# Row standard deviation: hand synchronisation, a ScalarE loop, aligned code, new last pieces and a VectorE transpose

## Chip, cores and metric

One core of one Trainium2 chip. The metric is the device time of one execution in microseconds (us), given as a median over several executions. Each execution also has a span, from its first to its last instruction as the profiler records it. In the two kernels compared the time is 1.7 to 2 us longer than the span, and that difference will matter. One execution per run was kept as a full profile. All executions compared here were classed as fast, except two single looks, whose state is unknown, as that of a single execution on one core always is.

## The reference

```python
# x: 8192 x 8192 float32, normally distributed
def reference(x):
    return np.std(x, axis=1)
```

The input is 268.4 MB, the output 32 KB. The kernel reads the input once.

## The kernel before

Thirty groups of 256 rows, 64 KB per partition each, pass through three buffers. VectorE sums each row, ScalarE squares and sums it. The last group and the four last blocks of 128 rows are divided otherwise: ScalarE takes 3072 columns of each row, VectorE makes batch-norm statistics of the rest. In the very last block, of which ScalarE takes 2048 columns, the input arrives in seven pieces, so that little work is left when the last byte lands. In the list of pieces, each pair is (columns that arrive, columns of them for ScalarE). A framework puts in all the waits. The parts that matter here:

```python
    for g in range(G - 1):
        xt = bulk.tile([P, 2 * C], FP32, name="xt")
        nc.sync.dma_start(out=xt, in_=xg[g])
        nc.vector.reduce_sum(out=s_all[:, 2 * g:2 * g + 2],
                             in_=xt.rearrange("p (j m) -> p j m", j=2),
                             axis=mybir.AxisListType.X)
        for j in range(2):
            squash(xt[:, j * C:(j + 1) * C], C, ACTF.Square, q_all[:, 2 * g + j:2 * g + j + 1])


    H = C // 2
    pieces = [(2048, 512), (2048, 512), (2048, 1024), (1024, 0), (512, 0), (256, 0), (256, 0)]
    # ... loads of the last group (xt_l), of rows 1 and 2 (xt_a), of row 3 in two halves ...
    c0 = C
    for n, _ in pieces:
        nc.sync.dma_start(out=xt_b[:, c0:c0 + n], in_=xt_rows[0][:, c0 - C:c0 - C + n])
        c0 += n
    # ... statistics of those rows; GpSimd joins the shares; TensorE transposes the results ...
    c0, k, j = C, 0, 0
    for n, a in pieces:
        src = xt_b[:, c0:c0 + n]
        if a:
            cnt, mean, m2v = (tri[:, 3 * j + i:3 * j + i + 1] for i in range(3))
            nc.gpsimd.memset(cnt, float(a))
            squash(src[:, 0:a], a, ACTF.Copy, mean, scale=1.0 / a)
            squash(src[:, 0:a], a, ACTF.Square, q_p[:, j:j + 1])
            # ... GpSimd turns ScalarE's two sums into (count, mean, squares) ...
        k = bn_cols(tri[:, 3 * n_act:], k, src[:, a:n])
        c0 += n

    nc.vector.bn_aggr(out=fin[:, 0:2], in_=tri)
    ps_t = psum.tile([TR, P], FP32)
    nc.tensor.transpose(ps_t, fin[:, 1:1 + TR], ident)
    std_t = stats.tile([TR, P], FP32)
    nc.scalar.activation(out=std_t, in_=ps_t, func=ACTF.Sqrt)
    nc.scalar.dma_start(out=out_t, in_=std_t)
```

## Time and profile before

| | before |
|---|---|
| time, first session, as it stood when the prediction was made | 630.96 us median of 3 (630.87 to 631.29) |
| span of the profiled execution (its time: 631.55 us) | 629.7 us |
| input queue, share of the 16 DMA engines | 98.8% |
| VectorE, ScalarE busy | 86%, 71% |

The page of the kernel before, first part: span, busy time and share of each engine, busy tenths of the DMA engines in 40 slices, and the DMA queues.

```profile
span 629.7 us, 466 instructions
...
PE 1.0 (0%) x3; PEld 0.2 (0%) x3; DVE 539.3 (86%) x99; ACT 449.4 (71%) x157; POOL 7.3 (1%) x44
...
DMA  9999999999999999999999999999999999999995
...
q1 hardware_dynamic: 5949, 268.47, 98.8%
q14 instruction: 4, 0.03, 0.0%
```

The input stream is what bounds the kernel: the DMA row is nine or more in every slice but the last. Queue 14 carries instructions. It has four packets in the span.

The chain of waits of the kernel before, in order of time (start, duration, what), beginning and end:

```profile
0.81 0.41 SPq L75
...
1.27 40.79 DMA xt<-in_x_dram
...
42.08 17.23 DVE s_all L76
...
59.37 41.02 DMA xt<-in_x_dram
...
584.49 37.31 DMA xt<-in_x_dram
...
621.83 1.29 DVE tri L68 x2
...
623.12 2.54 DVE tri L68 x5
...
625.76 0.56 DVE fin L187
...
626.36 0.39 PE ps_t L189
...
626.77 0.27 ACT std_t L191
```

A load takes 41 us from issue to landing because another, of 19.35 us, is served before it. A VectorE link of the chain only says which buffer came free; the DMA engines do not run dry meanwhile. From 621.83 us on it is different: VectorE works without a wait to 625.66, and then the output chain runs (aggregate, TensorE transpose, ScalarE square root).

The timeline of the kernel before, at its start and its end (start, duration, engine, line, operation; in brackets the idle time before and what ended it):

```profile
0.81 39.57 SPq L75 DMA_DIRECT2D xt<-in_x_dram  x4
0.87 0.06 DVE L49 MEMSET warm<- 128x1 f32 x1 [0.87 <-PEq L207]
...
22.75 17.22 DVE L76 TENSOR_REDUCE s_all<-xt 128x2 f32<-128x16384 f32 x1 [21.82 <-DMA xt<-in_x_dram]
...
42.08 17.22 DVE L76 TENSOR_REDUCE s_all<-xt 128x2 f32<-128x16384 f32 x1 [2.12 <-DMA xt<-in_x_dram]
...
621.83 3.82 DVE L68 BATCH_NORM_STATS2 tri<-xt 128x6 f32<-128x512 f32 x7 [0.42 <-DMA xt<-in_x_dram]
...
625.76 0.55 DVE L187 BATCH_NORM_AGGREGATE fin<-tri 128x2 f32<-128x87 f32 x1
...
627.07 0.55 ACTq L192 DMA_DIRECT2D out_dram<-std_t  x1
```

The first load is issued at 0.81 us, and the last store at 627.07, 2.64 us before the span ends.

Under the views lie the records of single DMA packets and landings. A load of 128 partitions runs on 16 engines and has 16 landings (those of the first load of the kernel before lie between 22.09 and 22.72 us); the kernel waits for all of them. For the argument below, the last landing is the one that counts. "Eighth landing" is the eighth of the 16 in order of time and stands for a typical engine.

### The profile page before, as it was taken

The page shows a single profiled execution, that of the slowest core. Times are in us where ns is not written, and L with a number is a line of the kernel's source. Part 1 is how long each engine was busy: PE and PEld are TensorE (multiplying, and loading weights), DVE is VectorE, ACT ScalarE, POOL GpSimd, SP SyncE. Part 2 cuts the span into 40 slices and gives each one's busy share as a digit, 9 for nine tenths or more (in the row PEclk, how much of TensorE's full clock was granted, in tenths as well). Part 3 has the DMA queues.
Part 4 walks back from the last instruction along what each step waited for, and adds up shares of the span by engine and source line. Part 5 has one row for each costly group of instructions (what it writes and reads, how often), then busy time and mean ns, then how long its engine had stood idle before and what let it go on. Part 6 is the DMA issues. An engine that isn't in the chain of part 4 may idle for free.

```text
span 629.7 us, 466 instructions
## 1 busy us (share of the span) xinstructions
PE 1.0 (0%) x3; PEld 0.2 (0%) x3; DVE 539.3 (86%) x99; ACT 449.4 (71%) x157; POOL 7.3 (1%) x44
## 2 busy tenths in 40 slices
PE   0000000000000000000000000000000000000000
PEld 0000000000000000000000000000000000000000
DVE  0588988889988889888898888998888988889897
ACT  0566886667966669766688666796666976668885
POOL 0000000000000000000000000000000000000002
DMA  9999999999999999999999999999999999999995
GB/s 400 408 458 404 462 400 466 400 466 400 466 400 466 400 466 400 466 400 466 400 466 400 466 400 466 400 466 404 462 412 454 416 450 429 437 437 429 419 411 240
DMA packets 5961, 268.50 MB, mean 426 GB/s; under 512 B 675, under 2 KB 965, under 8 KB 1221
## 3 DMA queue, kind: packets, MB, share of 16 engines
q1 hardware_dynamic: 5949, 268.47, 98.8%
q14 instruction: 4, 0.03, 0.0%
q10 hardware_dynamic: 8, 0.00, 0.0%
HBM read 268.44 MB, written 0.03 MB: 426 GB/s over the span
## 4 chain that ended last, share of the span: by engine, by line
DMA 71%; DVE 28%; SPq 0%; issue 0%; PE 0%; ACT 0%; DVEq 0%
DMA xt<-in_x_dram 71%; DVE s_all L76 27%; DVE tri L68 1%; SPq L95 0%; SPq L92 0%; SPq L75 0%; DVE fin L187 0%; PE ps_t L189 0%; ACT std_t L191 0%; DVEq L187 0%
## 5 line engine op out<-in xcount | busy, mean ns | idle before, releaser
L76 DVE TENSOR_REDUCE s_all<-xt 128x2 f32<-128x16384 f32 x29 | 499.4, 17220 | 82.3 <-DMA xt<-in_x_dram 82.3
L63 ACT ACTIVATE dump<-xt 128x8192 uint8<-128x8192 f32 (+4 forms) x76 | 440.4, 5794 | 174.3 <-DMA xt<-in_x_dram 173.0
L68 DVE BATCH_NORM_STATS2 bn<-xt 128x6 f32<-128x512 f32 x50 | 30.1, 675 | 3.1 <-DMA xt<-in_x_dram 3.1
L63 ACT ACTIVATION_READ_ACCUMULATOR dump<-xt 128x1 f32 x76 | 14.2, 186 | 0.0
L68 DVE BATCH_NORM_STATS2 tri<-xt 128x6 f32<-128x512 f32 (+1 forms) x13 | 7.4, 635 | 0.4 <-DMA xt<-in_x_dram 0.4
L106 POOL TENSOR_TENSOR m<-s_all 128x58 f32<-128x58 f32 x1 | 0.3, 282 | 581.3 <-DVE s_all L76 581.3
L120 DVE BATCH_NORM_AGGREGATE agg<-bn 128x2 f32<-128x60 f32 x5 | 2.1, 425 | 0.2
L191 ACT ACTIVATE std_t<-ps_t 4x128 f32<-4x128 f32 x1 | 0.3, 266 | 2.6 <-PE ps_t L189 2.6
L50 ACT ACT_TABLE_LOAD x1 | 1.3, 1283 | 0.8 <-PEq L207 0.8
L148 PE MATMUL ps_g<-ident,vN 128*30 128x128 f32 x2 | 0.6, 410 | 600.0 <-POOL vN L137 600.0
L49 DVE MEMSET warm<- 128x1 f32 x1 | 0.1, 59 | 0.9 <-PEq L207 0.9
L187 DVE BATCH_NORM_AGGREGATE fin<-tri 128x2 f32<-128x87 f32 x1 | 0.5, 548 | 0.1
L176 POOL TENSOR_TENSOR m_p<-tri 128x1 f32<-128x1 f32 x3 | 0.6, 193 | 0.8 <-ACT dump L63 0.8
L178 POOL TENSOR_TENSOR tri<-q_p,m_p 128x1 f32<-128x1 f32 x3 | 0.6, 189 | 1.2 <-ACT dump L63 1.1
L177 POOL TENSOR_TENSOR m_p<-m_p,tri 128x1 f32<-128x1 f32 x3 | 0.6, 190 | 0.2
L189 PE MATMUL ps_t<-ident,fin 128*4 128x128 f32 x1 | 0.4, 373 | 25.8 <-DVE fin L187 25.8
L152 ACT ACTIVATE std_g<-ps_g 30x128 f32<-30x128 f32 x2 | 0.4, 256 | 0.0
L159 POOL TENSOR_TENSOR s_all<-s_all,s_half 128x1 f32<-128x1 f32 x1 | 0.2, 190 | 17.7 <-ACT dump L63 17.7
L129 POOL TENSOR_TENSOR ug<-agg 128x2 f32<-128x2 f32 x1 | 0.2, 194 | 13.9 <-DVE agg L120 13.9
L148 PEld LDWEIGHTS ps_g<-ident,vN 128*30 128x30 f32 x2 | 0.1, 114 | 600.0 <-POOL vN L137 600.0
L108 POOL TENSOR_TENSOR vN<-q_all,m 128x58 f32<-128x58 f32 x1 | 0.3, 307 | 0.1
L173 POOL MEMSET tri<- 128x1 f32 x3 | 0.3, 98 | 0.0
(30 smaller groups left out, 5.3 us busy)
## 6 DMA issues: line engine op xcount, KB each, us to landing
xt<-in_x_dram SPq DMA_DIRECT2D x2, 4096.0 KB, 36.0
xt<-in_x_dram SPq DMA_DIRECT2D x2, 2048.0 KB, 29.0
xt<-in_x_dram SPq DMA_DIRECT2D x3, 1024.0 KB, 36.3
xt<-in_x_dram SPq DMA_DIRECT2D x1, 512.0 KB, 38.1
xt<-in_x_dram SPq DMA_DIRECT2D x30, 40.8
xt<-in_x_dram SPq DMA_DIRECT2D x1, 256.0 KB, 29.3
xt<-in_x_dram SPq DMA_DIRECT2D x2, 128.0 KB, 17.3
out_dram<-std_g SPq DMA_DIRECT2D x1, 30.0 KB, 10.2
```

The source lines that it names most:

```text
L50: nc.scalar.activation(out=warm, in_=warm, func=ACTF.Sqrt)
L63: nc.scalar.activation(out=dump[:, 0:n], in_=src, func=func, scale=scale, accum_out=acc)
L68: nc.vector.bn_stats(out=bn[:, k * SD:(k + 1) * SD], in_=src[:, d0:min(n, d0 + F)])
L76: nc.vector.reduce_sum(out=s_all[:, 2 * g:2 * g + 2], in_=xt.rearrange("p (j m) -> p j m", j=2), axis=mybir.AxisListType.X)
L120: nc.vector.bn_aggr(out=agg[:, r, :], in_=bn)
L148: nc.tensor.transpose(ps_g[:, j, :], vg[:, :, j], ident)
L152: nc.scalar.activation(out=std_g[:, :, j], in_=ps_g[:, j, :], func=ACTF.Sqrt, scale=1.0 / N)
L176: nc.gpsimd.tensor_mul(m_p[:, j:j + 1], mean, mean)
L177: nc.gpsimd.tensor_mul(m_p[:, j:j + 1], m_p[:, j:j + 1], cnt)
L178: nc.gpsimd.tensor_sub(m2v, q_p[:, j:j + 1], m_p[:, j:j + 1])
L187: nc.vector.bn_aggr(out=fin[:, 0:2], in_=tri)
L189: nc.tensor.transpose(ps_t, fin[:, 1:1 + TR], ident)
```

## The change

The intent: take instruction fetches out of the input stream (ScalarE loops over the groups, and the code of ScalarE and VectorE is aligned by `addr_align(128)`), end with less work after the last byte (new pieces), and shorten the output chain (VectorE transposes the last block's result instead of TensorE). For the loop, all the waits are written by hand. The diff is 439 lines; its core, with cuts marked and three comments added:

```diff
+    ctx.enter_context(tc.tile_critical())       # hand-synchronised from here
+    std_kernel(ctx, tc.nc, x, out)
 ...
+    for eng in (nc.vector, nc.scalar):
+        eng.addr_align(128, offset=0, max_nops=0)
 ...
-    pieces = [(2048, 512), (2048, 512), (2048, 1024), (1024, 0), (512, 0), (256, 0), (256, 0)]
+    pieces = [(3072, 768), (1536, 1024), (1024, 0), (1024, 512), (512, 0), (512, 0), (512, 0)]
 ...
-        for j in range(2):
-            squash(xt[:, j * C:(j + 1) * C], C, ACTF.Square, q_all[:, 2 * g + j:2 * g + j + 1])
+    with nc.scalar.Fori(0, LOOPS * 2 * NBUF, 2 * NBUF) as col:
+        for b in range(NBUF):
+            nc.scalar.wait_ge(token, 1)
+            nc.scalar.nop().then_inc(token, -1)
+            for j in range(2):
+                squash(buf[b][:, j * C:(j + 1) * C], C, ACTF.Square,
+                       q_all[:, bass.ds(col + (2 * b + j), 1)]).then_inc(row_done, 1)
+                nc.scalar.wait_ge(row_done, 1)
+                nc.scalar.nop().then_inc(row_done, -1)
+            nc.scalar.nop().then_inc(squared, 1)
 ...
+    for g in range(G - 1):                      # TensorE passes on landed data and free buffers
+        ...
+        T.need(V, v_group[g])
+        ...
+        nc.tensor.nop().then_inc(free, 1)
 ...
-    nc.vector.bn_aggr(out=fin[:, 0:2], in_=tri)
-    ps_t = psum.tile([TR, P], FP32)
-    nc.tensor.transpose(ps_t, fin[:, 1:1 + TR], ident)
-    std_t = stats.tile([TR, P], FP32)
-    nc.scalar.activation(out=std_t, in_=ps_t, func=ACTF.Sqrt)
-    nc.scalar.dma_start(out=out_t, in_=std_t)
+    # rows 1 to 3 are transposed, rooted and stored before this point
+    aggregated(fin[:, 0:2], tri)
+    V.need(V, V.n)
+    v_fin = V.did(nc.vector.transpose(out=tr, in_=fin[:, 1:33]))
+    A.need(V, v_fin)
+    A.did(nc.scalar.activation(out=std_l, in_=tr, func=ACTF.Sqrt))
+    A.need(A, A.n)
+    nc.scalar.dma_start(out=out_l, in_=std_l[0:P:32, :]).then_inc(done_l, 16)
+    nc.sync.wait_ge(done_g, 16)
+    nc.sync.wait_ge(done_t, 16)
+    nc.sync.wait_ge(done_l, 16)
```

## The prediction

> **What bounds it now.** The input stream. The slice table shows the 16 DMA engines nine tenths or more busy in all slices but the last; queue 1 alone takes 98.8% of them. In the packet records data moves from 1.83 to 624.03 us of the 629.7 us span: 268.4 MB in 622.2 us, 431 GB/s.[...] A 64 KB packet takes 2.420 us; 256 per engine make 619.5 us. The chain of waits names VectorE for 27%, but each reduce only frees a buffer 41 us before its load lands, while one group is served in 19.4 us, so the queue never runs dry. VectorE (17.2 us) and ScalarE (14.5 us per group) have slack. The body can gain 2.7 us at most.
>
> **What can move, term by term.**
> 1. *Instruction fetches.* ScalarE's unrolled code is 195 executed compute instructions and waits; queue 14 carries 8 KB instruction packets of 0.31-0.32 us at 251, 606 and 635 us (trace time; span time is about 11.3 less). Each delays one saturated DMA engine. In the landing times of the last piece 14 engines finish by 634.62, one at 634.93, one at 635.36: the straggler is 0.74 us late, and the lateness starts after the 251 us fetch (0.38 us at 305).[...] With the loop,[...] I expect these fetches to leave the stream: -0.6 us.[...]
> 2. *Last pieces.* Now VectorE ends its batch-norm statistics at 625.66, 1.56 us after the last landing (624.10), being 3.8 us behind from 621.83 without a wait. After: 12 instead of 13 of them, more of the row given to ScalarE early (768+1024+512 columns), 512-column last pieces. Replaying arrivals at 0.6 us per 512 columns VectorE ends about 0.9 us after the last landing: -0.6 us. GpSimd, waiting for ScalarE's third share, ends at about the same moment (+0.6 to +0.9), so it may become what ends last.
> 3. *Output chain.* From statistics to the store issue now 1.41 us (aggregate 0.55, PE 0.39, ScalarE 0.27, hops). The PE transpose gives way to a VectorE 128x32 transpose[...] and a self-wait; ScalarE square root about 0.2, plus a self-wait: about 1.1 us, -0.3 us. The store has 128-byte rows instead of 512: about 0 to +0.1.
> 4. *Synchronisation.* An extra handshake and branch before SyncE's first load (now at 0.81 us): +0.15 us, directly on the stream. Another collection of all engines after the last store: +0.25 us.
> 5. Buffer release through TensorE and ScalarE's loop waits: 0, there is over 10 us of slack.
>
> Sum: about -1.1 to -1.2 us. **Predicted 629.8 us, range 628.7 to 631.0**; faster by over 2% 0.01, within 2% 0.98, slower 0.01.
>
> **What would show it.** First load issue near 0.95 us instead of 0.81; instruction packets absent between 20 and 600 us; the spread of the last piece's 16 landings below 0.45 us instead of over 1.1; VectorE's last statistics about 0.9 us after the last landing; aggregate end to store issue 0.5 us instead of 0.75; from store issue to end of span 2.8-2.9 instead of 2.64.
>
> **What would make it wrong.** Fetches triggered by every loop iteration or alignment jump (each 0.3 us on one DMA engine, up to +3 us); a slower entry or exit of the hand-synchronised section (over 0.5 us each); GpSimd or ScalarE ending the last row late.

What is cut there are reasons and figures that no trace of this case shows: a ceiling for the stream, a reason for expecting the fetches to leave it, a word on branches, and the author's figure for VectorE's transpose inside the 1.1 us of term 3. The -0.6 us of term 1 is thus the author's estimate from the 0.74 us of the straggler. Each of the six terms of the sum stands. They add up to -1.0 to -1.1 us, the recorded sum says -1.1 to -1.2. The "about 0 to +0.1" for the store was an estimate without a run behind it. Of the three fetches named, two lengthened a data packet of the kernel before (by 0.38 us at 240 us, by 0.66 at 594); the third, at 623.65 us, did not widen the spread of the landings (0.95 us in the piece before the last, 0.93 in the last).

## The result

| | before | after |
|---|---|---|
| time, first session (one execution of the kernel before was added) | 630.94 us median of 4 (630.87 to 631.29) | 631.03 us median of 4 (630.97 to 631.24) |
| span of the profiled execution | 629.7 us | 629.2 us |
| time of that same execution | 631.55 us | 630.97 us |

The ratio after to before is 1.0001, with a 95% interval of 0.9983 to 1.0018. A ratio here is the mean time of one kernel's fast runs over that of the other's of the same rounds, so it is not quite the ratio of the medians. The change is worth nothing, and the time lies 0.03 us above the predicted range of 628.7 to 631.0.

The page of the changed kernel, the same lines as before:

```profile
span 629.2 us, 676 instructions
...
PE 1.0 (0%) x3; PEld 0.2 (0%) x3; DVE 539.1 (86%) x98; ACT 450.1 (72%) x158; POOL 7.4 (1%) x45
...
DMA  9999999999999999999999999999999999999996
...
q1 hardware_dynamic: 5955, 268.47, 98.9%
q14 instruction: 2, 0.02, 0.0%
```

The chain of waits of the changed kernel, its beginning and end:

```profile
1.47 41.26 DMA x<-in_x_dram
...
617.64 7.11 DVE tri L204 x12
...
624.85 0.53 DVE fin L210
...
625.40 0.22 DVE tr L306
...
625.65 0.23 ACT std_l L308
```

The timeline of the changed kernel at its start and its end:

```profile
1.01 40.06 SPq L126 DMA_DIRECT2D x<-in_x_dram  x4
...
23.41 17.22 DVE L159 TENSOR_REDUCE s_all<-x 128x2 f32<-128x16384 f32 x1 [23.41 <-DMA x<-in_x_dram]
...
42.76 17.22 DVE L159 TENSOR_REDUCE s_all<-x 128x2 f32<-128x16384 f32 x1 [2.13 <-DMA x<-in_x_dram]
...
625.91 1.11 ACTq L310 DMA_DIRECT2D out_dram<-std_l  x1
```

What the reader is to see: the first load is issued at 1.01 instead of 0.81 us, the first reduce starts 0.66 us later (23.41 against 22.75), and two instruction packets are still there. VectorE has no wait from 617.64 to 624.75, 0.91 us earlier than before; the output chain is a little shorter; but the issue of the last store takes 1.11 us instead of 0.55, and the span ends 3.34 us after its start instead of 2.64.

The two profiles, cut at points that both have (us from the span's start; the first packet and the landings are from the packet records, "last landing" is that of the last input piece):

```
                               before    after   difference of the stretch
first packet of the input        1.83     2.04   +0.21
last landing of the input      624.43   624.02   -0.62
VectorE ends its statistics    625.66   624.75   -0.50
last store, issue starts       627.07   625.91   -0.25
receipt of the last store      628.27   627.56   +0.45
end of the span                629.71   629.25   +0.25
                                                 sum -0.46
```

So by the profiles the span fell by 0.46 us, and yet the median time did not fall. The profiled execution of the kernel before took 631.55 us, more than any of its four timed ones. That had to be looked at first.

### The profile page after: what moved, and what is told of

Read it like the earlier page. It is cut to its first block, busy times and chain, and to the rows that moved or that the text cites. A ratio compares the mean times of both kernels' runs of the same rounds, so it can differ in the third digit from the quotient of the medians.

```text
span 629.2 us, 676 instructions
## 1 busy us (share of the span) xinstructions
PE 1.0 (0%) x3; PEld 0.2 (0%) x3; DVE 539.1 (86%) x98; ACT 450.1 (72%) x158; POOL 7.4 (1%) x45
## 4 chain that ended last, share of the span: by engine, by line
DMA 70%; DVE 29%; SPq 0%; issue 0%; PEldq 0%; ACT 0%; DVEq 0%
DMA x<-in_x_dram 70%; DVE s_all L159 27%; DVE tri L204 1%; SPq L132 0%; PEldq L198 0%; DVE fin L210 0%; SPq L126 0%; ACT std_l L308 0%; DVE tr L306 0%; SPq L339 0%; DVEq L100 0%; SPq L23 0%
## 5 line engine op out<-in xcount | busy, mean ns | idle before, releaser
L159 DVE TENSOR_REDUCE s_all<-x 128x2 f32<-128x16384 f32 x29 | 499.4, 17220 | 83.2 <-DMA x<-in_x_dram 83.2
L165 ACT ACTIVATE dump<-x 128x8192 uint8<-128x8192 f32 (+5 forms) x76 | 440.8, 5800 | 172.5 <-ACTq L173 148.4
L204 DVE BATCH_NORM_STATS2 bn<-x 128x6 f32<-128x512 f32 x50 | 30.1, 675 | 2.8 <-DMA x<-in_x_dram 2.8
L165 ACT ACTIVATION_READ_ACCUMULATOR dump<-x (+1 forms) x76 | 14.2, 186 | 0.0
L204 DVE BATCH_NORM_STATS2 tri<-x 128x6 f32<-128x512 f32 (+1 forms) x12 | 7.1, 659 | 0.2 <-DMA x<-in_x_dram 0.2
```

The costliest lines, as they stand in the source:

```text
L159: v_group.append(V.did(nc.vector.reduce_sum(out=s_all[:, 2 * g:2 * g + 2], in_=buf[g % NBUF].rearrange("p (j m) -> p j m", j=2), axis=AX)))
L165: return nc.scalar.activation(out=dump[:, 0:n], in_=src, func=func, scale=scale, accum_out=acc)
L204: V.did(nc.vector.bn_stats(out=bn[:, k * SD:(k + 1) * SD], in_=src[:, d0:min(n, d0 + F)]))
```

## The experiments

Twelve runs, none refused. "Spans" are those of all timed executions of a run. Over three later sessions the unchanged kernel before, timed 32 times, had spans from 629.0 to 629.9 with a mean of 629.41 us, and a mean time of 631.32 us.

### 1. The kernel before once more (before_again)

No edit.

> The kernel before, unchanged, to learn its spread. In the first profiles the span fell by 0.46 us (629.71 to 629.25) while the time did not (630.94 to 631.03). Theory A (the profile of before was a slow sample; its own run took 631.55): the spans of the runs here lie near 629.2, time minus span is about 1.75 us as for the changed kernel, and in a typical profile fewer instruction fetches fall on the slowest DMA engine, so that the last landing of the input is nearer 624.0 than 624.43 us. Theory B (the profile was typical and the changed kernel pays about 0.5 us after its last instruction): spans near 629.7, time minus span about 1.2.

Median 631.54 us of 5 (631.01 to 631.67); ratio to the kernel before of the same rounds 0.9999. The five spans are 629.7, 629.6, 629.1, 629.6 and 629.1. Theory A holds for the spans: the same kernel makes 629.1 or 629.7. Neither theory had the other number: time minus span is 1.92 us on average for the kernel before and 1.74 for the changed one, so something after the last instruction is 0.18 us shorter after the change. The profile here was again a slow one (629.70), and it repeats the first profile almost exactly: fetches at 240 and 596 us, last landing at 624.39.

### 2. The last store from SyncE (store_sp)

```diff
-    A.need(A, A.n)
-    nc.scalar.dma_start(out=out_l, ...)
+    nc.sync.wait_ge(A.sem, a_l)
+    nc.sync.dma_start(out=out_l, ...)
```

> The changed kernel with its last store issued from SyncE instead of ScalarE. In the changed kernel the issue of that store takes 1.11 us against 0.55 before, and its data moves 1.27 us after the start of the issue against 0.79. Theory A (the cost is ScalarE's: its queue, or its code at that place): the issue falls to about 0.3-0.45 us as for the two other stores, the span falls by about 0.4 us. Theory B (the cost is the store's shape, 4 rows of 128 bytes from every 32nd partition): still about 1.1 us, span unchanged or 0.1 longer for the hop.

Median 630.96 us of 5 (630.90 to 631.13), ratio 0.9994 (0.9981 to 1.0008). The timeline of this run:

```profile
625.74 0.23 ACT L308 ACTIVATE std_l<-tr 128x32 f32<-128x32 f32 x1 [1.91 <-DVE tr L306]
626.00 0.61 SPq L310 DMA_DIRECT2D out_dram<-std_l  x1
```

The issue got shorter (0.61 us), as theory A said, but the data did not move sooner: 1.24 us from the start of the issue to the first packet, against 1.27 in the changed kernel and 0.79 before. The receipt came 1.63 us after the start of the issue (1.65 and 1.20). Theory B is right in what counts. The duration of the issue is not the cost to read; the time to the first packet is.

### 3. ScalarE unrolled, alignment kept (unrolled)

```diff
-    LOOPS = (G - 1) // NBUF
+    LOOPS = 0
-    with nc.scalar.Fori(...) as col: ...
```

> The changed kernel with ScalarE's loop unrolled again, alignment kept: 212 instruction words instead of 113. If the loop is what keeps instruction fetches out of the stream, one or two 8 KB packets come back between 100 and 620 us, each makes one DMA engine 0.3-0.4 us late, and the last landing of the input is up to 0.4 us later (spread of the last piece over 0.7 us against 0.40). Rival: fetches do not matter, the 16 landings of the last piece stay within 0.5 us, the time is the same.

Median 631.50 us of 5 (631.34 to 631.61), ratio 1.0002. A packet of 8 KB came at 506.65 us. The next groups show what it does:

```
last landing of       group 0   group 12   group 29   last piece   spread of the last piece
after                   23.38     255.75     584.71      624.02      0.40
unrolled                23.62     255.84     585.20      624.50      1.13
```

(Spread: the last of the 16 landings less the eighth.) The expectation holds: one fetch in the stream, one engine about 0.4 us late from there on, the last landing 0.48 us later. Yet the spans are 629.1 to 629.4, no longer than those of the changed kernel: from the receipt of the last store to the end of the span there are 1.32 us here and 1.69 there. In exchange the time is 2.22 us longer than the span instead of 1.74, with a fetch at 630.38, after the last instruction. Why the end is cut differently was not found; the time counts both. Against the kernel before of the same rounds the mean time is 0.17 us longer here, and 0.05 longer and 0.14 shorter in the two runs of the changed kernel, which were timed in other sessions. The nearest neighbour is store_sp: it has the loop, ran in the same rounds, and differs from the changed kernel only in the engine that issues the last store. All its five times (630.90 to 631.13) lie below the five here (631.34 to 631.61), by 0.49 us in the means. So the loop is worth 0.1 to 0.5 us beside its own unrolled form; that it is worth anything beside the kernel before is another question, taken up below.

### 4. The loop without the alignment (noalign)

```diff
-    for eng in (nc.vector, nc.scalar):
-        eng.addr_align(128, offset=0, max_nops=0)
```

> The changed kernel without the alignment of ScalarE's and VectorE's code. If the two fetches at 2.6 and 5.1 us come from entering an aligned block, they vanish or move, the first group's spread falls from 0.78 us to about 0.33, and the first group lands about 0.4 us earlier;[...] one or two packets appear later in the stream with 0.3-0.4 us on one engine each. Rival (alignment does nothing): fetches at the same places, same landings.

(The cut takes out the condition under which packets were to appear later, a mechanism that no run shows.)

Median 631.26 us of 5 (631.14 to 631.43), ratio 1.0000. The spread of group 0 fell from 0.78 to 0.14 us. The first reduce in its timeline:

```profile
22.84 17.22 DVE L157 TENSOR_REDUCE s_all<-x 128x2 f32<-128x16384 f32 x1 [22.84 <-DMA x<-in_x_dram]
```

The line of the instruction queue on its page (packets, megabytes, share):

```profile
q14 instruction: 2, 0.02, 0.0%
```

The first reduce starts at 22.84 instead of 23.41 us. The same two packets exist, but at 594 and 600 us instead of 2.6 and 5.1:

```
last landing of       group 0   group 29   row block 1   last piece
after                   23.38     584.71      604.14       624.02
noalign                 22.81     584.00      604.31       624.18
```

Up to group 29 this kernel is 0.71 us ahead of the changed one (0.57 us from group 0, the rest from a loss that section 10 describes). The two fetches then take it all back. That is the central result for the fetches: alignment did not remove them, it moved them to the start of the stream. There they delay the slowest engine by 0.57 us at group 0, against the 0.87 us that noalign loses to the changed kernel between group 29 and the last piece. The lateness is still there at the end: in after_again the last landing is 0.99 us behind the eighth at group 10 and 0.95 us at the last piece. In time it is less settled: the mean here is 0.28 us above that of store_sp in the same rounds, and 0.03 us below that of the kernel before. A gain of up to 0.3 us by the alignment is not excluded.

### 5. The transpose on TensorE again (pe_store)

```diff
-    v_fin = V.did(nc.vector.transpose(out=tr, in_=fin[:, 1:33]))
-    A.need(V, v_fin)
-    A.did(nc.scalar.activation(out=std_l, in_=tr, func=ACTF.Sqrt))
+    T.need(V, v_fin)
+    t_l = T.did(nc.tensor.transpose(ps_l, fin[:, 1:2], ident))
+    A.need(T, t_l)
+    A.did(nc.scalar.activation(out=std_l, in_=ps_l, func=ACTF.Sqrt))
-    nc.scalar.dma_start(out=out_l, in_=std_l[0:P:32, :])    # 4 rows of 128 bytes
+    nc.scalar.dma_start(out=out_l, in_=std_l)               # 1 row of 512 bytes
```

> The changed kernel with the last block's result transposed on TensorE again (one row of 128, stored as one row of 512 bytes), all else kept. The last store's start of issue to the first packet of its data took 1.27 us in the changed kernel (4 rows of 128 bytes from every 32nd partition) and 0.79 before (4 rows of 512 bytes from neighbouring partitions); moving it to SyncE left it at 1.24. Theory A (the strided 4-row shape costs about 0.45 us): here it is 0.8 us or less, the chain from the last statistics to the issue grows from 1.16 to about 1.4 us, and the span is 0.1 to 0.2 us below the changed kernel's, so VectorE's transpose lost more in the store than it won in the chain. Rival (the entry of hand-synchronised code, or ScalarE's position after its loop, makes the store slow): 1.2-1.3 us here too and the span 0.25 longer.

Median 630.78 us of 5 (630.55 to 630.84), ratio 0.9988 (0.9974 to 1.0002); spans 628.8 to 629.1. Every one of the five times lies below all nine of the kernel before in the same rounds (631.16 to 631.74). The end of its timeline:

```profile
625.02 0.52 DVE L210 BATCH_NORM_AGGREGATE fin<-tri 128x2 f32<-128x81 f32 x1
...
625.60 0.37 PE L306 MATMUL ps_l<-ident,fin 128*1 128x128 f32 x1 [4.54 <-DVE fin L210]
626.01 0.27 ACT L308 ACTIVATE std_l<-ps_l 1x128 f32<-1x128 f32 x1 [2.10 <-PE ps_l L306]
626.30 0.50 ACTq L310 DMA_DIRECT2D out_dram<-std_l  x1
```

The first packet of the store moved at 627.05, 0.75 us after the start of the issue, and the receipt came 1.11 us after that start (1.65 in the changed kernel). The chain from the last statistics (624.92) to the issue took 1.38 us. VectorE's transpose had saved 0.2 us of the chain and lost 0.5 us in the store. Theory A holds.

### 6. No transpose at all (direct_store)

```diff
-    v_fin = V.did(nc.vector.transpose(out=tr, in_=fin[:, 1:33]))
-    A.did(nc.scalar.activation(out=std_l, in_=tr, func=ACTF.Sqrt))
+    A.did(nc.scalar.activation(out=std_l, in_=fin[:, 1:2], func=ACTF.Sqrt))
-    nc.scalar.dma_start(out=out_l, in_=std_l[0:P:32, :])
+    nc.scalar.dma_start(out=out_l, in_=std_l)               # 128 rows of 4 bytes
```

> The changed kernel without any transpose for the last block: square root of the 128x1 column on ScalarE and a store of 128 single words. The chain from the last statistics to the issue should fall from 1.16 to about 0.9 us. If a store's delay grows with the number of rows, the delay from issue to data is over 1.3 us and receipt is later than the 0.35 us seen so far, span equal or longer; if only the odd partition stride was dear, 0.8 us and the span is 0.6 us shorter than the changed kernel's.

Median 636.56 us of 5 (636.17 to 636.69), ratio 1.0080 (1.0066 to 1.0093): slower by 0.8%, which is clear of the noise. The issue began at 625.74 us and the first packet moved at 626.62, 0.88 us later. All packets had passed at 626.81. But the receipt came at 633.21, 6.40 us later, where stores of rows of 128 or 512 bytes had it 0.3 us after their last packet. Of the wait that ended the kernel this line of the waits of SyncE's queue tells (total, times, longest, us):

```profile
SPq L310 <- DMA out_dram<-std_l: 9.1, 1, 9.1
```

The expectation had named a late receipt as one outcome, but not its size, and it had tied it to a late first packet. That did not come: rows of 4 bytes from neighbouring partitions had their first packet after 0.88 us, nearly as early as rows of 512 bytes (0.79), and rows of 128 bytes from every 32nd partition only after 1.27. This speaks for the partition step, and against the length of the rows, as the cost of the changed kernel's store; a store that differs in the step alone was not run. The late receipt was seen with single words alone, as rows of 128 bytes had theirs 0.31 us after the last packet; what causes it these runs do not show.

### 7. Only the new pieces (tile_pieces), and once more (tile_pieces_again)

```diff
-    pieces = [(2048, 512), (2048, 512), (2048, 1024), (1024, 0), (512, 0), (256, 0), (256, 0)]
+    pieces = [(3072, 768), (1536, 1024), (1024, 0), (1024, 512), (512, 0), (512, 0), (512, 0)]
```

> The kernel before with only the new list of last pieces. Theory: VectorE ends its statistics about 0.75 us after the last landing of the input (1.23 in the two profiles of the kernel before, 0.73 in the changed one), so spans are 0.5 us below those of the kernel before in the same rounds, with the same cluster of fast and slow runs. Rival (the lag comes from the hand synchronisation): no gain.

> The kernel before with only the new pieces, once more: 0.7 to 0.9 us under the kernel before of the same rounds. Rival: the first result (630.56) was luck in where the fetches fell (its profile had group 29 landed at 584.21, that of the kernel before at 584.75 and 584.69); then the gain is only the lag of VectorE, 0.5 us.

First run: median 630.56 us of 5 (630.40 to 631.25), ratio 0.9988 (0.9975 to 1.0002), beside 631.16 to 631.74 for the kernel before. Second: median 630.94 of 5 (630.60 to 631.06), ratio 0.9995 (0.9981 to 1.0009), beside 630.93 to 631.57. The chain of the first:

```profile
617.44 7.14 DVE tri L68 x12
...
624.68 0.53 DVE fin L187
...
625.67 0.27 ACT std_t L191
```

VectorE ended at 624.58, 0.72 us after the last landing (623.86), where it had been 1.23. That is the 0.5 us of the theory. The rival of the second run is right about the rest: the first run's 0.75 us contained luck. Its profile had group 29 landed at 584.21, the second one's at 584.67. The two runs together average 630.80 us against 631.32 for the 18 runs of the kernel before beside them: 0.5 us. Neither interval excludes 1, so what is shown firmly is the shorter lag in the profiles; the gain in time agrees with it.

### 8. New pieces, no transpose, framework waits (tile_direct)

```diff
+    # pieces as above; rows 1 to 3 transposed, rooted and stored before the last aggregate
     nc.vector.bn_aggr(out=fin[:, 0:2], in_=tri)
-    nc.tensor.transpose(ps_t, fin[:, 1:1 + TR], ident)
-    nc.scalar.activation(out=std_t, in_=ps_t, func=ACTF.Sqrt)
-    nc.scalar.dma_start(out=out_t, in_=std_t)
+    nc.scalar.activation(out=std_l, in_=fin[:, 1:2], func=ACTF.Sqrt)
+    nc.scalar.dma_start(out=out[T0:T0 + P].rearrange("(p i) -> p i", i=1), in_=std_l)
```

> The kernel before with the new pieces, the three other rows' results stored early as in the changed kernel, and the last block's column stored directly. It keeps the first load at 0.81 us and the short exit (1.44 us from the receipt of the last store to the end of the span, 1.69 in the changed kernel). If my ledger is right the span is that of the kernel before less 0.5 (pieces) less about 0.5 (no transpose): about 1.0 us less, plus whatever the store of 128 words costs. That would beat both kernels: about 630.2 us.

Median 636.69 us of 5 (636.09 to 636.88), ratio 1.0079. My hoped-for best version was the worst, for the reason of direct_store: last packet at 626.74, receipt at 633.21, the framework's waits notwithstanding.

### 9. The changed kernel once more (after_again)

No edit.

> The changed kernel unchanged, beside the next run on one chip, so that both are compared in the same rounds. If the change as a whole is worth nothing and its new pieces alone are worth 0.8 us, this run is 0.4 to 0.6 us slower than the next and within 0.3 us of the kernel before. Its two early instruction fetches should again fall on the slowest engine: group 0's last landing near 23.4-23.7 us, group 29's near 584.7-584.9, as in the four profiles with aligned code so far.

Median 631.04 us of 5 (630.85 to 631.41), ratio 0.9998 (0.9985 to 1.0012). Group 0 landed at 23.58 and group 29 at 584.78 us, as expected. The distance to tile_pieces_again is 0.1 us in the medians and 0.17 in the means, less than the 0.4 to 0.6 expected; with spreads of this size it can't be told from the expected one.

### 10. Two more looks at the kernel before (before_look1, before_look2)

No edit.

> One more profile of the kernel before. Its spans form a range from 629.1 to 629.9 with nothing changed. Theory: what differs is which DMA engine an instruction fetch delays. In a profile with a span near 629.2 the landing of group 29 is near 584.2 us, in one near 629.7 it is near 584.7. Rival: the spread comes from elsewhere (the end of the program, the store), with group 29 at 584.7 either way.

> The same look again, for a second sample: group 29's last landing and the span should move together, 584.2 with 629.2 and 584.7 with 629.7.

631.21 and 631.49 us, spans 629.28 and 629.65. The expected pair of numbers came out, and more with it:

```
                    eighth landing       last landing                                      span
                    group 0   group 10   group 10  group 12  group 29  last piece
before                22.39     216.46     216.70    255.79    584.75      624.43        629.71
before_look1          22.41     215.91     216.34    255.12    584.07      623.92        629.28
before_look2          22.30     216.39     216.69    255.67    584.64      624.34        629.65
tile_pieces           22.34     215.87     216.24    255.24    584.21      623.86        628.61
after                 22.61     216.56     217.04    255.75    584.71      624.02        629.25
after_again           22.62     216.11     217.10    255.80    584.78      624.09        629.32
```

Two things vary from one execution to the next. The fetch at 240 us costs the last landing 0.3 to 0.4 us in the other profiles of this code but 0.08 in before_look1 (38.78 us from group 10 to group 12, against 39.09 before; ten groups without a disturbance take 193.50, two take 38.70). And in some profiles all 16 engines lose about 0.5 us together between group 1 and group 10: 194.07 us in the kernel before, 193.50 in before_look1. Both kernels have it at times (after: 193.95, after_again: 193.49). So my theory, that only the engine hit by a fetch matters, was half of it. In the changed kernel the common loss did not show in the last landing, as the eighth engine lost 0.45 us and the slowest engine, already late, only 0.16. What causes the common loss stays open; nothing in the traces names it. It came in four of the seven profiles with the code of the kernel before and in one of the seven hand-synchronised ones, too few to say whether the change makes it rarer.

So profiles have to be compared without it. The stretch from the first packet to the last landing of the input, in profiles whose eighth landings show no common loss (193.49 to 193.59 us from group 0 to group 10):

```
code of the kernel before      before_look1 622.08   tile_pieces 622.02   tile_direct 622.22
loop and alignment             after_again  622.04   store_sp    622.08   direct_store 622.09   pe_store 622.16
loop, no alignment             noalign      622.14
alignment, no loop             unrolled     622.46
```

The two kernels are the same here to 0.1 us (the means of the first two lines are 622.11 and 622.09). The packet records fit this. A fetch lengthens one data packet, the one that starts as the fetch ends: by 0.3 to 0.4 us at 240, 506 and 600 us, by 0.53 at 5.1 to 5.4 us and by 0.66 at 594 (against the median packet of its size). Both kernels have two fetches inside the stream, at 240 and 594 to 596 us before, at 2.0 to 2.6 and 5.1 to 5.4 us after (the first of these falls where all packets are still slow from the start, so its cost was not separated); the packet at 623.65 us in the kernel before did not widen the spread of the landings (0.95 us in the piece before the last, 0.93 in the last). Only unrolled has three, and it alone stands out.

The two profiles that the account below rests on, first before_look1 (page, chain of waits, timeline):

```profile
span 629.3 us, 466 instructions
...
622.68 2.54 DVE tri L68 x5
...
626.64 0.55 ACTq L192 DMA_DIRECT2D out_dram<-std_t  x1
```

The same of after_again:

```profile
span 629.3 us, 676 instructions
...
617.70 7.11 DVE tri L204 x12
...
625.97 1.11 ACTq L310 DMA_DIRECT2D out_dram<-std_l  x1
```

Without the common loss the spans are the same: VectorE ends 0.41 us earlier in the changed kernel and the store is issued 0.67 us earlier, and the store and the exit take 0.70 us longer.

## Why the prediction was wrong

The prediction was 629.8 us, a gain of 1.1 to 1.2. In the same rounds the medians moved by +0.09 and by -0.16 us. Term by term, with the two first profiles, with all profiles (four of the kernel before, two of the changed kernel), and with the one profile of each that has no common loss (before_look1 and after_again):

| term | predicted | first pair | all profiles | without the common loss |
|---|---|---|---|---|
| entry, first packet | +0.15 | +0.21 | +0.21 | +0.21 |
| instruction fetches, first packet to last landing | -0.6 | -0.62 | -0.43 | -0.04 |
| VectorE's lag behind the last landing | -0.6 | -0.50 | about -0.5 | -0.58 |
| output chain to the issue | -0.3 | -0.25 | -0.25 | -0.25 |
| last store, issue to receipt | 0 to +0.1 | +0.45 | +0.45 | +0.45 |
| exit | +0.25 | +0.25 | +0.25 | +0.25 |
| sum, span | -1.1 to -1.2 | -0.46 | about -0.3 | +0.04 |
| after the span (time minus span) | not named | -0.18 in the means | -0.18 | -0.18 |

(The predicted terms as written add up to -1.0 to -1.1; the 0.1 us is a slip.)

1. **What bounds the kernel** was right: the stream. Undisturbed groups follow each other at 19.35 us in every profile, 8.39 MB each, which is 434 GB/s.

2. **The step that failed first was "Instruction fetches: ... I expect these fetches to leave the stream: -0.6 us".** It had the right mechanism and the wrong consequence. A fetch does make one saturated engine late, by 0.3 to 0.7 us where it could be read, and the loop does remove one from mid-stream (unrolled shows it back at 506.65 us). But two remain, as many as the kernel before had between the start of the stream and its last pieces, and alignment only moved them to 2.6 and 5.1 us, inside the stream; noalign has them at 594 and 600. Without the common loss the term measures -0.04 us instead of -0.6. Read only by its absence "between 20 and 600 us", the forecast would even have passed; its other sign, a spread of the 16 landings below 0.45 us from first to last, did not come (0.57 in the first profile, 1.11 in after_again). The price of the early fetches is in group 0, which lands at 23.38 to 23.67 us with alignment and 22.81 without.

3. **The first-pair figure of that term looks right by luck.** The lateness that it was to remove (0.74 us in the prediction; 0.92 to 1.03 in the four profiles of the kernel before, as the last less the eighth landing) is still 0.95 us in after_again. What differed in the first pair was the common loss of about 0.5 us that comes and goes. The profile of the kernel before had it on all engines, so its span was 629.71 us where 32 executions average 629.41. In the first profile of the changed kernel the slowest engine, already late, took only 0.16 us of it. The four spans of the changed kernel in the first session average 629.33: against 629.41 only 0.08 us of span is left.

4. **"The store has 128-byte rows instead of 512: about 0 to +0.1" was mis-sized.** It measured +0.45 us, in the time from issue to first packet (1.27 against 0.79), not in the writing. store_sp and pe_store show that it belongs to the store of four rows from every 32nd partition, not to ScalarE's queue nor to hand-written waits. The early first packet of direct_store (0.88) points to the partition step and not to the row length, but no run separates the two alone. It more than eats the 0.25 us that VectorE's transpose won.

5. **VectorE's lag** was nearly right in its gain (-0.6 predicted, -0.5 measured), though I had read the last landing from the piece before the last (624.10 instead of 624.43), so the lag before was 1.23 and not 1.56 us. tile_pieces shows that the pieces alone bring it. GpSimd ended at 624.38, before VectorE, so it did not become the end.

6. **Entry and exit** came as costed: 0.21 and 0.25 us. They are read from traces (first load at 0.81 us in all profiles with framework waits, 1.01 in all hand-synchronised ones), not from an experiment of their own. **Fetches at every turn of the loop**, the first risk named, did not come: no packet of code lies between 5.14 us and the end of the span in the changed kernel, over nine turns of the loop.

7. The sum: without the common loss the span terms add up to +0.04 us (629.28 to 629.32). With -0.18 after the span, whose cause was not found, that makes -0.14 in time, where the measured medians moved by +0.09 and -0.16. The mean of the 32 later executions of the kernel before and that of all nine of the changed kernel differ by 0.26 (631.32 and 631.06); one session differs from another by as much. The expected gain went to two places: the fetches that moved instead of leaving (0.56) and the store (0.4).

No version here is shown to beat the kernel before, though three runs lie below it: the kernel before with the new pieces alone (630.56 and 630.94 us in its two runs) and the changed kernel with the TensorE transpose (630.78) are 0.3 to 0.9 us below the kernel before of the same rounds in the medians, less than 0.2%, and their intervals include no difference. With one edited line the former has all of the gain that could be traced to a cause, the 0.5 us of VectorE's lag; the hand synchronisation adds nothing that these runs could resolve.

## What to carry to other kernels

In this saturated DMA stream an instruction packet made one engine late whether it fell at 5 us (0.53 us on one data packet) or at 600 (0.3 to 0.4), so shifting fetches brought no gain that the landings show: count them, and look at the last of the 16 landings, not at the mean. Time a small store by its receipt, not by its issue or its packets: here an unhandy shape cost 0.45 us before its first packet and single words 6.4 us after their last. When the gain in question is below the spread of single executions, profile both kernels more than once, and compare profiles that have the same disturbances.
